# MLP down projection: from 7 products over 2x2 blocks to 20 products over 3x4 by 4x2 blocks, with the weight sums on POOL

## The chip, the cores and the metric

The kernel runs on one NeuronCore of a Trainium2 chip. The metric is the device time of one execution in microseconds (us). The core has a matmul engine (PE; its weight loads are listed as PEld), a vector engine (DVE), a scalar engine (ACT), a general engine (POOL) and SyncE (SP), which issues most of the DMA transfers. Each engine works through its own instruction list in order, and semaphores tie the lists together.

## The reference, cut to what matters

The reference is one step of a small streaming encoder with two layers: 1024 prompt tokens and 8 x 16 = 128 sample tokens, model width 1024, MLP width 4096, all in float32. Each layer has attention and then an MLP with a residual:

```python
def mlp(x, g_norm, w_up, w_down):
    return jnp.square(jax.nn.relu(rmsnorm(x, g_norm) @ w_up)) @ w_down
...
        hp = hp + mlp(hp, g_mlp[layer], w_up[layer], w_down[layer])
        hs = hs + mlp(hs, g_mlp[layer], w_up[layer], w_down[layer])
```

`hp` holds the prompt tokens (eight tiles of 128, numbered 0 to 7), `hs` the sample tokens (one tile, called ST). The change concerns the last product, (1152 tokens x 4096) @ (4096 x 1024), and the form in which its left operand is stored.

## The kernel before, in words

Every float32 product is made of three matmuls on operands that were split in two parts, hi and lo (`mm3`, L725-729: hi x hi, hi x lo, lo x hi). A split (`split`, L106-115) is a cast on ACT (L109) that writes hi, and a subtraction on DVE (L115) that writes lo = value - hi.

Both MLP projections run over blocks with a fast 2x2 scheme: seven block products stand in for eight, at the price of sums of blocks ahead of them (on tokens and on weights) and sums of products behind them. The sample tile is outside the scheme and has plain products.

*Up projection* (`mlp_up`, L759-886). Sixteen blocks of 256 hidden columns. Per block, seven products of 12 matmuls over 512 tokens each, in banks X, Y, Z of PSUM, 24 matmuls for the sample tile, and two transposes of the sample's result. ACT and DVE turn the banks into four quadrants of activations (`e`, tiles named `hc`: hidden half x token half, 128 x 512 each). `combos` (L718-723) makes four sums of quadrants on DVE, and POOL's queue stores seven token operands in DRAM (`hd`, L886), and the sample's split transpose (`h8d`, L825).

*Down projection* (`mlp_down`, L888-1105). Four stages of four blocks each. In a stage, SP loads four raw weight quarters (tiles `r`, 128 x 2048, L949-959) and seven token operands (tiles `s`, three buffers), each of which is split by ACT and DVE. DVE makes four sums of weight quarters in place (L1061, L1063, L1076, L1093). The split weights lie in `w`, three buffers. A product is 4 token tiles x 4 k x 3 = 48 matmuls of 512 columns; the sample tile adds four products of 12 matmuls a stage. Results go from PSUM to the residual tiles `x` by DVE additions (L1033). In the last stage tiles 0 to 3 and ST are stored after the third pair of products, and tiles 4 to 7 after the last product. Layer 0 stores them in `xd`, from where the next layer's attention loads them.

The order of the instructions on each engine comes from a scheduler that sorts by dependencies, buffers and priorities; `follow` and `behind` pin the order of PE's products and of the first loads of a down projection. The first loads have raised priority, so that they go out during the up projection's last blocks. In the down projection PE, ACT, DVE and SP work; POOL has nothing to do there.

Of the kernel before, what the change touches and what calls it, by code (L numbers as in the profile page):

```python
# [8 lines left out]
F32 = mybir.dt.float32  # L9
# [21 lines left out]
HB = 11  # L31
RORDER = (0, 1, 5, 2, 3, 6, 4)
# [43 lines left out]
class Build:  # L76
# [682 lines left out]
    def mlp_up(self, layer, sx, x8, rp, raw0):  # L759
        nc = self.nc  # L760
        tt = nc.vector.tensor_tensor
        with ExitStack() as st:
# [56 lines left out]
            def turn(b, h8):  # L819
# [3 lines left out]
                h8t = hp.tile([P, 2, 2, P], F32R, tag="h8t", name="h8t")  # L823
# [3 lines left out]
            def tokens(blk, quad, ws, e, c, with_sample):  # L827
                w = c.stop - c.start
                v = [z[:, c] for z in e]
# [33 lines left out]
                if with_sample:  # L863
                    turn(blk, h8)
# [10 lines left out]
            for b in range(NFB):  # L875
                quad, ws = weights(b)
                e = [hp.tile([P, 512], F32, tag="h", name="hc", bufs=HB) for _ in range(4)]
                if b == 0:
                    tokens(b, quad, ws, e, slice(0, 256), False)
                    tokens(b, quad, ws, e, slice(256, 512), True)  # L880
                else:
                    tokens(b, quad, ws, e, slice(0, 512), True)
                s = [hp.tile([P, 512], F32, tag="h", name="hs", bufs=HB) for _ in range(3)]
                self.combos(*e, [s[0], s[1], e[2], s[2]])
                for p, z in enumerate((e[0], e[1], e[3], s[0], s[1], e[2], s[2])):
                    nc.gpsimd.dma_start(self.hd[b // 4][:, p, b % 4], z)  # L886

    def mlp_down(self, layer, out):  # L888
        nc = self.nc
        tt = nc.vector.tensor_tensor  # L890
        wd = self.ins["w_down"][layer].rearrange("(b h p) n -> h p b n", h=2, p=P)
        with ExitStack() as st:
            self.psum_pools(st, f"dn{layer}", dict(y=(4, 1), x=(4, 1)), dict(x="x", y="y"))
            kinds = dict(
                s=([P, 2, 4, 512], F32R), w=([P, 2, 4, 512], F32R), h=([P, 4, 2, 2, P], F32R),
                r=([P, 4, 512], F32), p=([P, 4, D], F32),
            )
            homes = {}
# [5 lines left out]
            slots = {}  # L904

            def place(name, *tags, side=None):
                pool = self.pool(st, f"d{name}{layer}", side=side)
                for t in tags:
                    homes[t] = pool
                    slots[t] = fresh(t)  # L910

# [3 lines left out]
            for n, tags in enumerate((("p0",), ("w2",), ("s2",), ("r5", "r6"), ("h8",), ("s1",), ("w1",), ("s0",))):  # L915
                place(f"e{n}_", *tags, side="right")
            place("a", "w0", "r1")
            place("b", "r2")
            place("c", "r3")
            place("d", "r4")  # L920
            xp = self.pool(st, f"dx{layer}")
            xs = {}
            for t in range(NT // 2, NT):
                xs[t] = xp.tile([P, D], F32, tag=f"x{t}", name="x")
            self.bias_tiles(xp)
            xp.tile([P, 504], F32, tag="pad", name="pad")
            place("g", "r0")
            yp = self.pool(st, f"dy{layer}")
            for t in (ST, 0, 1):
                xs[t] = yp.tile([P, D], F32, tag=f"x{t}", name="x")  # L930
            yp = self.pool(st, f"dz{layer}")
            for t in (2, 3):
                xs[t] = yp.tile([P, D], F32, tag=f"x{t}", name="x")

            self.pe = self.sp = None
            self.nr = 0

            def take_raw():
                self.nr += 1
                return take(f"r{RORDER[(self.nr - 1) % 7]}")  # L940

            N = [slice(0, 512), slice(512, 1024)]
            ns = NFB // 4
            count = 0
            for s in range(ns):
                b = [[None, None], [None, None]]
                svs = {}

                def load(dst, src):  # L949
                    a = nc.sync.dma_start(dst, src)  # L950
                    if s == 0:
                        if self.sp is not None:
                            self.behind(self.sp, a)
                        self.sp = a

                def load_b(h, n):
                    r = take_raw()
                    load(r, wd[h, :, s * 4 : s * 4 + 4, N[n]])
                    b[h][n] = r

                def load_s(p):
                    nonlocal count
                    z = take(f"s{count % 3}")
                    svs[p] = z, f"w{(count + (count >= 9) + (count >= 16)) % 3}"
                    count += 1
                    load(z[:, 1].bitcast(F32), self.hd[s][:, p])

                def wsplit(p, src):
                    w = take(svs[p][1])
                    self.cut = self.split(w[:, 0], w[:, 1], src)  # L970
                    return w[:, 0], w[:, 1]

                def ssplit(p):
                    z = svs[p][0]
                    self.cut = self.split(z[:, 0], z[:, 1], z[:, 1].bitcast(F32))
                    return z[:, 0], z[:, 1]

                def load_x(*ts):
                    for t in ts if s == 0 else ():
                        load(xs[t], self.xd[t])  # L980

                if layer == 0 and s == 1:
                    self.prep_bias(self.dp)
                def load_h():
                    h8 = take("h8")
                    for q in range(4):
                        load(h8[:, q].bitcast(F32), self.h8d[s * 4 + q])
                    return h8

                def early(n):  # L990
                    return self.tc.high_priority(n) if s == 0 else nullcontext()

                with early(EARLY[0]):
                    load_b(0, 0)
                    load_x(ST, 0, 1)
                with early(EARLY[1]):
                    load_b(1, 0)
                    load_s(0)
                with early(EARLY[2]):
                    load_s(1)  # L1000
                with early(EARLY[3]):
                    h8 = load_h()
                load_x(2, 3)
                load_b(0, 1)
                load_b(1, 1)
                load_s(4)
                load_x(*range(NT // 2, NT))

                def product(banks, w, sv, first, done):
                    for i in range(4):  # L1010
                        c = slice(i * P, i * P + P)
                        z = [
                            self.mm3(
                                banks[i], sv[0][:, k, c], sv[1][:, k, c], w[0][:, k], w[1][:, k],
                                first and k == 0, k == 3,
                            )
                            for k in range(4)
                        ]
                        self.follow(z[0][0], z[-1][1])
                        done(i)  # L1020

                def sample(ps, w, h, first, last):
                    z = [
                        self.mm3(
                            ps, h8[:, k, 0, h], h8[:, k, 1, h], w[0][:, k], w[1][:, k],
                            first and k == 0, last and k == 3,
                        )
                        for k in range(4)
                    ]
                    self.follow(z[0][0], z[-1][1])  # L1030

                def add(t, n, ps):
                    tt(xs[t][:, N[n]], ps, xs[t][:, N[n]], ALU.add)  # L1033

                def store(t):
                    if s == ns - 1:
                        nc.sync.dma_start(out(t), xs[t])

                bank = lambda role: self.psum(role, [P, 512], f"ps_{role}")
                X = [bank("x") for _ in range(4)]  # L1040
                w = wsplit(0, b[0][0])
                if s == 0:
                    self.behind(self.cut[0], self.marks[0])
                sv = ssplit(0)
                if s == 0:
                    self.behind(self.cut[0], self.marks[1])
                    self.behind(self.cut[1], self.marks[2])
# [33 lines left out]
                def third(i):  # L1081
                    add(i, 1, Y[i])
                    store(i)
# [723 lines left out]
```

## Time and profile before

| | us |
|---|---|
| median of 3 runs | 2393.08 |
| range of the runs | 2387.11 to 2398.38 |
| span of the profiled execution, first to last instruction | 2386.1 |
| time of the profiled execution itself | not listed apart; the lowest run is 1.0 above its span |
| DVE busy in the span | 1627.6 |
| ACT busy in the span | 1216.5 |
| POOL busy in the span | 540.8 |

The stages in the span, by the first matmul of each kind: the down projection of layer 0 begins at 802.2 us and that of layer 1 at 2033.2 us; attention of layer 1 lies between about 1150 and 1650 us. A row of a group of instructions reads: line of the kernel, engine, operation, output <- inputs, shapes, count | busy time in us, mean ns of one | idle time of the engine just ahead of them in us, and what ended it. A row of a timeline reads: start in us, duration in us, engine, line, operation, output <- inputs, shapes, count, and in brackets the idle time ahead of it. Matmul durations of 389 ns overlap, so PE's pace is read from the number of matmuls in a stretch.

### The profile page before, as it was taken

To read this page: it belongs to the slowest core of one execution; us is meant where nothing else is said; L and a number is where in the kernel's file an instruction comes from. 1 tells how busy PE (TensorE), PEld (TensorE's weight loads), DVE (VectorE), ACT (ScalarE), POOL (GpSimd) and SP (SyncE) were. 2 spreads that over 40 slices of the span, in tenths; PEclk is the share of its full clock that TensorE was granted. 3 is DMA by queue.
4 is the path that set the end of the run, shared out by engine and by line. 5 is a ranking of instruction groups with operands and counts; after the bars stand their busy time and mean duration, and the time that the engine had idled before them with its cause. 6 is when DMAs were issued, how large, how long until landed. Compare 5 with 4: busy or idle time off the path is not lost.

```text
span 2386.1 us, 33438 instructions
## 1 busy us (share of the span) xinstructions
PE 2313.9 (97%) x11621; PEld 1931.7 (81%) x11621; DVE 1627.6 (68%) x3002; ACT 1216.5 (51%) x2423; POOL 540.8 (23%) x828
## 2 busy tenths in 40 slices
PE   7998999899999999999999999998999999999999
PEld 6787877788888878888778788887888888888887
DVE  6788786655565776776577876877555565777674
ACT  3777674555555432332267666665555555323321
POOL 4334332311221100000333444444111211000000
PEclk9999999999999999999999999999999999999999
DMA  7335545343443964333653655554443445734332
GB/s 258 119 108 169 170 146 200 129 146 126 157 146 123 356 213 149 119 128 109 232 153 112 198 166 167 168 168 169 142 142 129 158 145 203 274 133 159 117 113 115
DMA packets 217529, 383.78 MB, mean 161 GB/s; under 512 B 50248, under 2 KB 124944, under 8 KB 210192
## 3 DMA queue, kind: packets, MB, share of 16 engines
q1 hardware_dynamic: 194288, 305.08, 38.9%
q0 software_dynamic: 21776, 71.84, 7.8%
q10 hardware_dynamic: 1296, 4.72, 0.5%
q8 instruction: 92, 1.51, 0.3%
q14 instruction: 77, 0.63, 0.1%
HBM read 245.42 MB, written 135.09 MB: 159 GB/s over the span
## 4 chain that ended last, share of the span: by engine, by line
PE 79%; DVE 7%; DMA 7%; ACT 3%; issue 2%; POOL 1%; SPq 1%; ACTq 0%; DVEq 0%; POOLq 0%
PE ps_x L727 9%; PE ps_x L729 9%; PE ps_x L728 9%; PE ps_y L729 7%; PE ps_y L728 7%; PE ps_y L727 7%; PE ps_mm L198 3%; PE ps_mm L200 3%; PE ps_mm L199 3%; PE ps_tr L305 2%; PE ps_mm L157 1%; PE ps_mm L158 1%; PE ps_mm L159 1%; PE ps_s L729 1%; PE ps_s L728 1%
## 5 line engine op out<-in xcount | busy, mean ns | idle before, releaser
L109 ACT CAST w<-r 128x2048 fp32r<-128x2048 f32 x56 | 107.1, 1913 | 325.2 <-PE ps_y L729 213.0
L727 PE MATMUL ps_x<-w,s 128*128 128x512 f32 x512 | 199.6, 390 | 4.2 <-DVE hc L866 2.1
L729 PE MATMUL ps_x<-w,s 128*128 128x512 f32 x512 | 199.4, 389 | 0.0
L728 PE MATMUL ps_x<-w,s 128*128 128x512 f32 x512 | 199.3, 389 | 0.0
L198 PE MATMUL ps_mm<-w,hh 128*128 128x512 f32 x432 | 172.5, 401 | 7.3 <-POOL w L166 3.2
L200 PE MATMUL ps_mm<-w,hl 128*128 128x512 f32 x432 | 172.1, 399 | 1.6 <-DVE hl L115 0.8
L199 PE MATMUL ps_mm<-w,hh 128*128 128x512 f32 x432 | 170.9, 397 | 1.3 <-DVE w L171 1.1
L109 ACT CAST s<-s 128x2048 fp32r<-128x2048 f32 x56 | 107.1, 1913 | 118.1 <-DMA s<-hd 109.3
L115 DVE TENSOR_TENSOR w<-r,w 128x2048 fp32r<-128x2048 f32 x56 | 128.2, 2290 | 51.0 <-ACT w L109 51.0
L727 PE MATMUL ps_x<-sx,w 128*128 128x512 f32 (+1 forms) x408 | 157.9, 387 | 3.9 <-ACT hc L846 3.0
L1033 DVE TENSOR_TENSOR x<-ps_y,x 128x512 f32<-128x512 f32 x136 | 92.4, 687 | 100.8 <-PE ps_y L729 100.8
L729 PE MATMUL ps_x<-sx,w 128*128 128x512 f32 (+1 forms) x408 | 154.2, 378 | 0.0
L728 PE MATMUL ps_x<-sx,w 128*128 128x512 f32 (+1 forms) x408 | 154.1, 378 | 0.0
L109 ACT CAST w<-ru 128x512 fp32r<-128x512 f32 (+1 forms) x160 | 110.0, 708 | 85.5 <-PE ps_y L728 32.0
L729 PE MATMUL ps_y<-w,s 128*128 128x512 f32 x384 | 149.5, 389 | 0.0
L727 PE MATMUL ps_y<-w,s 128*128 128x512 f32 x384 | 149.4, 389 | 0.0
L728 PE MATMUL ps_y<-w,s 128*128 128x512 f32 x384 | 149.4, 389 | 0.0
L115 DVE TENSOR_TENSOR s<-s 128x2048 fp32r<-128x2048 f32 x56 | 128.0, 2286 | 29.1 <-ACT s L109 28.9
L115 DVE TENSOR_TENSOR ptl<-ps_tr,pth 128x512 fp32r<-128x512 f32 x180 | 122.5, 685 | 24.1 <-ACT pth L109 17.8
L115 DVE TENSOR_TENSOR w<-ru,w 128x512 fp32r<-128x512 f32 (+1 forms) x160 | 126.5, 793 | 11.2 <-ACT w L109 11.1
L115 DVE TENSOR_TENSOR wq<-ru,wq 128x1024 fp32r<-128x1024 f32 x32 | 39.7, 1240 | 131.9 <-ACT wq L109 131.9
L109 ACT CAST pth<-ps_tr 128x512 fp32r<-128x512 f32 x180 | 104.9, 595 | 45.0 <-PE ps_tr L305 36.7
(280 smaller groups left out, 6579.7 us busy)
## 6 DMA issues: line engine op xcount, KB each, us to landing
s<-hd SPq DMA_DIRECT2D x56, 1024.0 KB, 4.7
ru<-in_w_up SPq DMA_DIRECT2D x64, 512.0 KB, 4.0
r<-in_w_down SPq DMA_DIRECT2D x32, 1024.0 KB, 5.8
hd<-hc POOLq DMA_DIRECT2D x128, 256.0 KB, 2.7
hd<-hs POOLq DMA_DIRECT2D x96, 256.0 KB, 2.5
x<-xd SPq DMA_DIRECT2D x41, 512.0 KB, 4.4
o<-oTd SPq DMA_DIRECT2D x52, 256.0 KB, 5.0
xd<-xo SPq DMA_DIRECT2D x18, 512.0 KB, 2.8
```

The costliest lines, as they stand in the source:

```text
L109: a = nc.scalar.copy(hi, src)
L115: return a, e.tensor_tensor(lo, src, hi.bitcast(F32), ALU.subtract)
L157: nc.tensor.matmul(ps, oh[:, k, :], w[:, 0, k, nn], start=(k == 0), stop=False)
L158: nc.tensor.matmul(ps, oh[:, k, :], w[:, 1, k, nn], start=False, stop=False)
L198: nc.tensor.matmul(ps, a, w[:, 0, k, :], start=(k == 0), stop=False)
L199: nc.tensor.matmul(ps, a, w[:, 1, k, :], start=False, stop=False)
L200: self.lp = nc.tensor.matmul(ps, b, w[:, 0, k, :], start=False, stop=(k == KC - 1))
L305: self.lp = nc.tensor.transpose(pt[:, i, :], get(i), self.ident)
L727: a = mm(ps, ah, bh, start=first, stop=False, skip_group_check=True)
L728: mm(ps, ah, bl, start=False, stop=False, skip_group_check=True)
L729: return a, mm(ps, al, bh, start=False, stop=last, skip_group_check=True)
L1033: tt(xs[t][:, N[n]], ps, xs[t][:, N[n]], ALU.add)
```

## The change: what it does

1. *The block product of the down projection.* The tokens are cut in three parts of three tiles, (5, 6, 7), (ST, 0, 1) and (2, 3, 4): the sample tile is now an ordinary tile. The hidden dimension is cut in four for each of two sets, the output columns in two. A set makes (3x4) by (4x2) blocks in 20 products where 24 would be plain. Each product is 3 token tiles x 4 k x 3 = 36 matmuls of 512 columns; 40 products a layer.
2. *Token operands.* The up projection writes the activations of a block into two tiles `eh` of 128 x 1152 (ST, then tiles 0 to 7); the sample's transposes are copied there by ACT. After an even block, `forms_even` makes 2 sums and stores 5 operands; after an odd block, `forms_odd` makes 16 sums and stores 15; each is 128 x 384. The sums write in place of tiles that were stored before, where they can. All stores stay on POOL's queue.
3. *Weight operands.* A product uses one raw weight block or the sum or difference of two (16 of 20 in a set). The sums are made on POOL into two buffers (`s0`, `s1`), or in place for the last four; there are two buffers for split weights (`w0`, `w1`), three for tokens (`a0` to `a2`), eleven for raw weights.
4. *Order and PSUM.* Products are grouped in chains (`CHAINS`) that accumulate in the same three banks. Between products of a chain the banks are read, with plus or minus, into the output blocks that need the value at that point. Ahead of the products a loop issues loads three products early, the splits one early, the weight sum two early.
5. *Memory.* The buffers of the down projection have a new fixed order in SBUF (`DOWN_HOME`).

The core of the diff (tables, `forms_odd` and the loading helpers shortened):

```diff
-HB = 11
-RORDER = (0, 1, 5, 2, 3, 6, 4)
+RANK = 20
+PARTS = ((5, 6, 7), (ST, 0, 1), (2, 3, 4))
+COLS = (2, 0, 1)
+W_FORMS = (
+    "+.......", ".......+", "+......-", ".+.....+", ".....+..",
...
+CHAINS = (
+    ((4,), (0, 10), (14, 15), (-13, 18), (12, 1, 2, 17, 9, 8), (-6, 5, 11, 3, 7), (16, 19)),
+    ((0,), (-4, 15), (-14, 10), (-13, 18), (19, 16), (12, 1, 2, 17), (-6, 5, 11, 7, 3), (9, 8)),
+)
...
-                self.split(h8t[:, 0], h8t[:, 1], t8)
-                nc.gpsimd.dma_start(self.h8d[b], h8t.bitcast(F32))
+                for h in range(2):
+                    nc.scalar.copy(eh[h][:, 0:P], t8[:, h])
...
-                s = [hp.tile([P, 512], F32, tag="h", name="hs", bufs=HB) for _ in range(3)]
-                self.combos(*e, [s[0], s[1], e[2], s[2]])
-                for p, z in enumerate((e[0], e[1], e[3], s[0], s[1], e[2], s[2])):
-                    nc.gpsimd.dma_start(self.hd[b // 4][:, p, b % 4], z)
+                if b % 2 == 0:
+                    even = eh
+                    self.forms_even(b // 2, eh)
+                else:
+                    self.forms_odd(b // 2, even + eh, hp.tile([P, 3 * 3 * P], F32, tag="h", name="ht", bufs=7))
...
+    def forms_even(self, c, eh):
+        tt, put = self.nc.vector.tensor_tensor, self.form_store(c)
+        a0, a4, a8 = self.form_cut(eh[0])
+        a1, a5, a9 = self.form_cut(eh[1])
+        put(18, a8)
+        put(3, a0)
+        put(13, a5)
+        tt(a4, a4, a8, ALU.add)
+        put(10, a4)
+        tt(a9, a5, a9, ALU.add)
+        put(11, a9)
...
+            def add_w(n):
...
+                x, y = (raws[used[i][0]] for i in (0, -1))
+                if len(used) == 1:
+                    assert g == 1
+                    src[n] = x
+                    return
+                src[n] = x if n >= total - TAIL + 2 else take(f"s{n % 2}")
...
+                nc.gpsimd.tensor_tensor(src[n], x, y, ALU.add if plus else ALU.subtract)
+
+            def split_w(n):
...
+                w = ws[n] = take(f"w{n % 2}")
+                self.split(w[:, 0], w[:, 1], src.pop(n))
+                a = aa[n]
+                self.split(a[:, 0], a[:, 1], a[:, 1].bitcast(F32))
...
+            add_w(0)
+            split_w(0)
+            add_w(1)
+            for n, (s, p, g, first, final, reads, _) in enumerate(seq):
...
+                split_w(n + 1)
+                add_w(n + 2)
+                if first:
+                    banks = [self.psum("c", [P, 512], "ps_c") for _ in range(3)]
+                a, w = aa.pop(n), ws.pop(n)
+                for i in range(3):
+                    c = slice(i * P, i * P + P)
                     z = [
                         self.mm3(
+                            banks[i], a[:, 0, k, c], a[:, 1, k, c], w[:, 0, k], w[:, 1, k],
+                            first and k == 0, k == 3,
                         )
                         for k in range(4)
                     ]
                     self.follow(z[0][0], z[-1][1])
+                    for o, v in reads:
+                        x = xs[PARTS[o // 2][i]][:, N[o % 2]]
+                        tt(x, x, banks[i], ALU.add if v > 0 else ALU.subtract)
```

More of the change, by code (lines that the diff above doesn't have):

```diff
@@ L863, in tokens @@
                 if with_sample:
-                    turn(blk, h8)
+                    turn(eh, h8)
                 product(Y, 2, False, True)
@@ L917, in mlp_down @@
[L917 to L930, printed above, removed]
@@ L931, in mlp_down @@
-            yp = self.pool(st, f"dz{layer}")
-            for t in (2, 3):
-                xs[t] = yp.tile([P, D], F32, tag=f"x{t}", name="x")
-            self.pe = self.sp = None
[L936 to L982, printed above, removed]
-                    self.prep_bias(self.dp)
[L984 to L1022, printed above, removed]
@@ new lines, in mlp_down @@
+            for n, tags in enumerate(DOWN_HOME):
+                pool = self.pool(st, f"d{n}_{layer}")
+                for t in tags.split():
+                    if t == "bias":
+                        self.bias_tiles(pool)
+                        pool.tile([P, 504], F32, tag="pad", name="pad")
+                    elif t[0] == "+":
+                        pool.tile([P, int(t[1:])], F32, tag="gap", name="gap")
+                    else:
+                        homes[t] = pool
+                        slots[t] = fresh(t)
@@ new lines, in mlp_down, with slot, load @@
+            total = len(seq)
+            left = {}
+            for n, (s, *_, reads, _) in enumerate(seq):
+                for i, _ in reads:
+                    left[i] = n
+            last = {i // 2: max(left[i], left[i ^ 1]) for i in left}
+            aa, ws = {}, {}
+            def slot(n):
+                return 1 + n % 2 if n >= total - TAIL else n % 3
+            def load(dst, src):
+                a = nc.sync.dma_start(dst, src)
+                if self.sp is not None:
+                    self.behind(self.sp, a)
+                self.sp = a
@@ L1030, in sample @@
                     self.follow(z[0][0], z[-1][1])
[L1032 to L1043, printed above, removed]
@@ L1069, in mlp_down @@
-                sv = ssplit(3)
-                s2 = bank("y")
-                sample(s2, w, 0, True, True)
-                add(ST, 1, s2)
-                Y = [bank("y") for _ in range(4)]
-                product(Y, w, sv, True, lambda i: add(i + 4, 1, Y[i]))
-                t4 = b[1][0]
-                tt(t4, b[1][0], t2, ALU.subtract)
-                load_s(6)
-                w = wsplit(6, b[1][1])
-                sv = ssplit(6)
-                def third(i):
-                    add(i, 1, Y[i])
-                    store(i)
@@ L1099, in mlp_down @@
-                sv = ssplit(2)
-                def fourth(i):
-                    add(i + 4, 0, X[i])
-                    store(i + 4)
-                product(X, w, sv, False, fourth)
+                    for o, v in reads:
+                        x = xs[PARTS[o // 2][i]][:, N[o % 2]]
+                        tt(x, x, banks[i], ALU.add if v > 0 else ALU.subtract)
+                    for part in {o // 2 for o, _ in reads}:
+                        if last[part] == n:
+                            t = PARTS[part][i]
+                            nc.sync.dma_start(out(t), xs[t])
@@ L1107, in bias_tiles @@
+                for m in range(n + 1, total):
+                    if m not in aa:
+                        if slot(m) in {slot(q) for q in range(n + 1, m)}:
+                            break
+                        load_h(m)
     def bias_tiles(self, pool):
```

201 lines of the change are left out of this document (137 added, 64 removed).

## The prediction

> **What bounds the kernel now.** I read the page first, then stretches of the down projection one by one, then the groups of instructions there.
>
> ```profile
> span 2386.1 us, 33438 instructions
> PE 2313.9 (97%) x11621; PEld 1931.7 (81%) x11621; DVE 1627.6 (68%) x3002; ACT 1216.5 (51%) x2423; POOL 540.8 (23%) x828
> ```
>
> PE is busy 97% of the span, but that is an average, and its 389 ns matmuls overlap. The two stretches of 200 us below lie inside the down projections of layer 0 and 1; columns are start:end, length, then busy time (count) of PE, PEld, DVE, ACT, POOL, granted clock, DMA share, GB/s.
>
> ```profile
> 900.00:1100.00 200.00, 200.00 (x884) 165.68 (x883) 139.58 (x118) 61.27 (x32) 0.00 (x0) 1.00 0.37 126
> 2090.00:2290.00 200.00, 200.00 (x884) 165.58 (x884) 143.27 (x119) 62.81 (x33) 0.00 (x0) 1.00 0.39 137
> PE ps_x L727 <- DVE x L1033: 2.0, 1, 2.0
> ```
>
> 884 matmuls in 200 us at clock 1.00 are 0.2262 us each: here PE issues without a gap, POOL does nothing, DVE is busy 70 to 72%. The last row, from the list of waits of layer 0's down projection, is PE's only wait in it, 2.0 us. So in this stage PE's matmul count is the time, as long as nothing else needs more than PE.
>
> ```profile
> L729 PE MATMUL ps_x<-w,s 128*128 128x512 f32 x512 | 199.4, 389 | 0.0
> L729 PE MATMUL ps_y<-w,s 128*128 128x512 f32 x384 | 149.5, 389 | 0.0
> L729 PE MATMUL ps_y<-w,h 128*128 128x512 f32 x128 | 49.8, 389 | 0.0
> ```
>
> L727, L728 and L729 have equal counts, so both layers issue 3 x (512+384+128) = 3072 matmuls, 1536 a layer: 347.5 us.
>
> **The change, part by part.**
>
> *Matmuls.* 40 products a layer (two sets of 20), each 3 token tiles x 4 k x 3 = 36 matmuls of the same shape: 1440. The built order of the changed kernel has 192 fewer for both layers. 192 x 0.2262 = **-43.4 us**, if PE stays fed. One product now lasts 36 x 0.2262 = 8.14 us instead of 10.86.
>
> *What feeds a product.* Durations:
>
> ```profile
> L115 DVE TENSOR_TENSOR w<-r,w 128x2048 fp32r<-128x2048 f32 x56 | 128.2, 2290 | 51.0 <-ACT w L109 51.0
> L115 DVE TENSOR_TENSOR s<-s 128x2048 fp32r<-128x2048 f32 x56 | 128.0, 2286 | 29.1 <-ACT s L109 28.9
> L1033 DVE TENSOR_TENSOR x<-ps_y,x 128x512 f32<-128x512 f32 x136 | 92.4, 687 | 100.8 <-PE ps_y L729 100.8
> L1033 DVE TENSOR_TENSOR x<-ps_x,x 128x512 f32<-128x512 f32 x128 | 87.0, 685 | 42.6 <-PE ps_x L729 42.0
> L1061 DVE TENSOR_TENSOR r<-r,r 128x2048 f32<-128x2048 f32 x8 | 18.3, 2283 | 0.0
> L720 DVE TENSOR_TENSOR hs<-hc 128x512 f32<-128x512 f32 x32 | 22.1, 692 | 70.6 <-ACT hc L801 70.6
> L109 ACT CAST w<-r 128x2048 fp32r<-128x2048 f32 x56 | 107.1, 1913 | 325.2 <-PE ps_y L729 213.0
> 919.21 1.91 ACT L109 CAST w<-r 128x2048 fp32r<-128x2048 f32 x1 [9.51 <-PE ps_y L729]
> 921.15 2.29 DVE L115 TENSOR_TENSOR w<-r,w 128x2048 fp32r<-128x2048 f32 x1 [1.25 <-ACT w L109]
> 923.36 0.68 DVE L1033 TENSOR_TENSOR x<-ps_x,x 128x512 f32<-128x512 f32 x1
> ```
>
> The timeline rows show that a successor starts 0.08 before the recorded end, so a weight split holds DVE 2.21, a PSUM read 0.61. From 512 to 2048 elements DVE grows by (2.286-0.692)/1536 = 1.038 ns an element, so a token split of 1536 takes 1.755 recorded, 1.68 in a row. Written out, the chains read the banks for 41 output blocks a layer, three tiles each: 123 reads (136 + 128 for both layers before, 132 a layer). DVE then needs 40 x (2.21+1.68) + 123 x 0.61 = 231 us a layer against PE's 325.8: 71%, as now. ACT needs 40 x (1.91+1.44) = 134 us, the 1.44 again by size. Neither is the bound by itself.
>
> *Sums on POOL.* Sixteen DVE sums a layer (L1061, L1063, L1076, L1093, 2.28 us) go; 32 sums of 128x2048 arrive on POOL, which before did nothing here. The trace has no POOL sum of that size; the nearest:
>
> ```profile
> L684 POOL TENSOR_TENSOR s<-x,s 128x512 f32<-128x512 f32 x6 | 7.7, 1286 | 0.1
> L550 POOL TENSOR_TENSOR uks<-kc,uks 128x128 fp32r<-128x128 f32 x32 | 16.7, 521 | 1.7
> ```
>
> (1.286-0.521)/384 = 1.99 ns an element gives 1.286 + 1536 x 1.99 ns = 4.35; I take 4.4. Ends: 2.28, DVE's own row for that shape, and 4 x 1.286 = 5.14, no fixed cost at all. The Trainium skill, GPSIMD Engine Reference, section 3.1, states 4497 ns for a fp32 sum of N=2048; by it the sum below would end some 5 us later.
>
> *What the two engines do to each other.* This decides the forecast. Around the first MLP's start both work on SBUF (POOL rows, then DVE rows, of the timeline):
>
> ```profile
> 411.50 1.76 POOL L683 TENSOR_TENSOR s<-x 128x512 f32<-128x512 f32 x1
> 414.98 1.29 POOL L684 TENSOR_TENSOR s<-x,s 128x512 f32<-128x512 f32 x1
> 422.56 1.30 POOL L681 TENSOR_TENSOR s<-x 128x512 f32<-128x512 f32 x1
> 423.81 2.28 POOL L683 TENSOR_TENSOR s<-x 128x512 f32<-128x512 f32 x1
> 412.02 0.68 DVE L665 TENSOR_TENSOR x<-ps_wo,x 128x512 f32<-128x512 f32 x1
> 415.05 2.30 DVE L622 SCALAR_TENSOR_TENSOR x<-x,mrs,gb 128x1024 f32<-128x1024 f32 x1
> 420.90 1.28 DVE L622 SCALAR_TENSOR_TENSOR x<-x,mrs,gb 128x1024 f32<-128x1024 f32 x1
> 422.69 2.24 DVE L622 SCALAR_TENSOR_TENSOR x<-x,mrs,gb 128x1024 f32<-128x1024 f32 x1
> ```
>
> L622 takes 1.28 alone. Begun at 415.05 under the POOL sum of 414.98 to 416.27 it ends at 417.35, 1.08 after POOL: it stood still until POOL was done. At 422.69 the same happens under the sum of 422.56, and then the next POOL sum, due at 423.81, stands until that DVE instruction ends at 424.93 and takes 2.28 in place of 1.29. The read of a PSUM bank at 412.02, with one SBUF input, runs at its 0.68 inside a POOL sum. So POOL's sum and a DVE instruction with two SBUF inputs exclude each other for their whole length; a blocked DVE instruction saves 0.2 of its start. The Trainium skill, SBUF — State Buffer, section "Who interferes with whom", makes it a rule: the two-input DVE instruction and a GpSimd instruction that reads SBUF hold a shared read port whole, first come; by it a sum of 2048 blocks as wholly as the 512 ones here, and the rows agree.
>
> Both splits on DVE have two SBUF inputs. In the changed build, DVE's order in a period is: weight split of product n+1, read of product n's first bank, token split of n+1, reads of banks two and three. POOL's sum for n+3 waits for just that weight split, because it frees one of two buffers (s0, s1). So POOL starts while DVE does the read, and the token split, which PE needs for n+1, stands behind the sum; behind it stand two thirds of the reads, and behind those the next weight split. With r output blocks read per tile, a period with a sum is 2.21 + 4.4 + 1.5 (1.68 less 0.2) + 2r x 0.61 = **8.1 + 1.2 r us** (for r = 0 the token split goes ahead of POOL, same sum), against PE's 8.14. Of the 40 products 8 have r = 0, 23 have r = 1, 9 have r = 2. Excess over PE if each period had a sum: 23 x 1.2 + 9 x 2.4 = 49 us; 32 of 40 do: **+39.4 us a layer**. Port time, 32 x 4.4 + 40 x 3.9 = 297 us, would fit under PE's 325.8; it is the order that costs.
>
> A layer's down projection: 325.8 + 39.4 = 365 for 347.5, +17.7; both, **+35 us**.
>
> *Sums of tokens in the up projection.* Per pair of blocks 18 sums of 128x384 (0.692 - 128 x 1.038 ns = 0.56) replace 8 of 0.69 and two 0.42 splits of the sample: +3.7 us of DVE in a pair, +59 for both layers.
>
> ```profile
> L115 DVE TENSOR_TENSOR h8t<-ps_t,h8t 128x256 fp32r<-128x256 f32 x32 | 13.4, 417 | 0.0
> 550.00:600.00 50.00, 50.00 (x247) 42.21 (x246) 27.93 (x43) 27.88 (x46) 9.77 (x18) 1.00 0.43 146
> hd<-hc POOLq DMA_DIRECT2D x128, 256.0 KB, 2.7
> s<-hd SPq DMA_DIRECT2D x56, 1024.0 KB, 4.7
> ```
>
> DVE is idle 22 of 50 us there under a full PE, which hides it: 0. Without that cover it is up to +59. Several new sums overwrite a tile that a store on POOL's queue must first have read (2.7 us to land); queued behind them are the next block's weight splits, which have until that block's end, and the 22 idle us are their slack. POOL issues 20 stores a pair for 16 now, idle otherwise. SP's loads: 40 of 768 KB for 28 of 1024, the weights' 16 unchanged; at 4.7 us for the bigger one, within an 8.14 us period: 0.
>
> *Ends of the stage.*
>
> ```profile
> 802.16 0.50 PE L727 MATMUL ps_x<-w,s 128*128 128x512 f32 x1 [1.06 <-DVE hc L866]
> ```
>
> The stage opens now after a 1.06 us wait. In the changed order two POOL sums lie among the last stores and DVE's last token sums: between 0 and 8.8 a layer, I take 3: +6. Tiles of layer 0 are stored from product 32 of 40 on, earlier than now: -2, between -5 and 0.
>
> **Sum.** 2386.1 + 35 + 6 - 2 = 2425 of span. No time of its own is given for the profiled execution; its span stands 7.0 below the runs' median of 2393.1. Forecast **2432 us**.
>
> **Rivals.**
> 1. *PE sets the pace* (the other side, faster). If POOL's sums run in DVE's gaps, 43 of gain less 4 at the ends leave 2354. It decides at a sum of T < 8.14-2.21-1.5-1.2 = 3.2 us, or if DVE's token split gets in before POOL. For: the port total fits. Against: both POOL rows point to 4.4, and the sum's release is the instruction just before. 0.17.
> 2. *Half absorbed*: sums slip into periods of single-term products and r = 0; excess 20 a layer, about 2393. 0.13.
> 3. *Heavier*: sums of 5.14 add 0.74 to each of 32 periods, +47, or the up projection loses part of its cover: 2480. 0.09.
> 4. *The product count does not fall*: excluded by the built order.
>
> **How the numbers follow.** Forecast 0.61, by itself 2410 to 2460 (sums of 4.0 to 4.8). The range leaves out rival 1 and the heaviest part of rival 3: 2385 to 2472. About 0.5% is what a measurement of this kernel tells from no change: faster 0.18, same 0.13, slower 0.69.
>
> **What would show it.** Right: 40 products of 36 matmuls, but some 790 matmuls in 200 us of the down projection, not 884; PE waiting there for DVE's token split, some 40 us a layer; that split recorded at 4 to 5 us on average in place of 1.76, the PSUM read still 0.69; POOL sums of 4.4 or longer. Wrong: 884 matmuls per 200 us and token splits near 1.8 (rival 1), POOL sums under 3.2, or PE waits in the up projection (rival 3).

## The result, and the profile after

The changed kernel takes 2471.68 us (median of 4 runs, 2465.16 to 2474.45) where the kernel before took 2394.69 on the same chip: 1.033 times as long, 95% interval 1.0304 to 1.0355. The forecast was 2432. The direction is as forecast, and so is the exclusion between POOL and DVE, but the loss is twice the size: +79 us at that ratio instead of +39. The time lies at the very end of the stated range of 2385 to 2472.

The head of the page, and below it the same two stretches of the down projections as before (same columns):

```profile
span 2472.3 us, 33316 instructions
...
PE 2311.3 (93%) x11429; PEld 1911.4 (77%) x11429; DVE 1848.3 (75%) x3128; ACT 1273.0 (51%) x2503; POOL 914.6 (37%) x956
```

```profile
900.00:1100.00 200.00, 178.56 (x767) 143.76 (x765) 184.09 (x105) 75.64 (x45) 101.09 (x20) 0.99 0.39 129
2090.00:2290.00 200.00, 175.11 (x722) 140.37 (x721) 172.28 (x117) 69.73 (x41) 88.07 (x27) 0.93 0.40 139
```

767 and 722 matmuls where 884 were; 790 had been forecast. DVE went from 70% to 92% busy in the first stretch with fewer instructions (105 for 118): they last longer. A look at each down projection from its first matmul to its last, in the same view, gives the whole loss:

```profile
803.60:1196.80 393.20, 343.70 (x1440) 274.72 (x1439) 340.56 (x238) 135.61 (x88) 183.39 (x60) 0.97 0.47 159
2079.10:2467.50 388.40, 346.32 (x1440) 278.54 (x1439) 335.81 (x216) 132.53 (x82) 173.59 (x46) 0.95 0.40 139
sum 781.60, PE 690.02 PEld 553.26 DVE 676.37 ACT 268.14 POOL 356.98; mean PE 345.01 PEld 276.63 DVE 338.19 ACT 134.07 POOL 178.49
```

The same view of the kernel before:

```profile
802.16:1150.20 348.04, 346.00 (x1528) 285.96 (x1528) 245.17 (x212) 101.39 (x56) 7.92 (x12) 1.00 0.47 165
2033.20:2381.50 348.30, 348.29 (x1536) 288.21 (x1536) 237.73 (x201) 100.49 (x54) 1.94 (x4) 1.00 0.41 148
```

So the two grew by 45.2 and 40.1, and the span by 86.2 (of the two profiled executions; the medians on one chip are 77 apart). Little else moved: the first down projection starts at 803.6 instead of 802.2.

The groups of instructions, shapes kept apart, and the list of PE's waits over the whole span (waited in total, times, longest):

```profile
L1067 POOL TENSOR_TENSOR s<-r,r 128x2048 f32<-128x2048 f32 x56 | 291.2, 5202 | 281.2 <-DVE w L134 160.4 <-DMA r<-in_w_down 116.7 <-PE ps_c L748 2.2
L134 DVE TENSOR_TENSOR a<-a 128x1536 fp32r<-128x1536 f32 x80 | 258.5, 3232 | 46.4 <-ACT a L128 46.4
L134 DVE TENSOR_TENSOR w<-s,w 128x2048 fp32r<-128x2048 f32 x56 | 176.3, 3150 | 21.8 <-ACT w L128 21.7
L1119 DVE TENSOR_TENSOR x<-x,ps_c 128x512 f32<-128x512 f32 x246 | 158.8, 676 | 35.7 <-PE ps_c L748 35.5
```

```profile
PE ps_c L746 <- DVE x L1119: 54.7, 25, 6.0
PE ps_c L747 <- DVE w L134: 23.9, 9, 4.2
...
PE ps_c L746 <- ACT a L128: 7.1, 4, 2.5
PE ps_c L748 <- DVE a L134: 5.4, 6, 1.1
```

A token split lasts 3.23 us on average instead of the 1.755 worked out for one alone, a weight split 3.15 instead of 2.29, and the PSUM read, with one input from SBUF, is unchanged at 0.676. That is the exclusion of the prediction, but not always at the place that it named, and so not the 4 to 5 us for a token split: in the timeline 34 of the 80 token splits last over 2.2 us, and 24 of the 80 weight splits over 2.6. But PE hardly waits for token splits (5.4 us); it waits for PSUM reads and weight splits, 78.6 us.

One period of it, DVE and then POOL in the timeline:

```profile
1043.57 5.45 DVE L134 TENSOR_TENSOR w<-s,w 128x2048 fp32r<-128x2048 f32 x1
1048.94 0.67 DVE L1119 TENSOR_TENSOR x<-x,ps_c 128x512 f32<-128x512 f32 x1
1049.54 5.80 DVE L134 TENSOR_TENSOR a<-a 128x1536 fp32r<-128x1536 f32 x1
1055.26 1.27 DVE L1119 TENSOR_TENSOR x<-x,ps_c 128x512 f32<-128x512 f32 x2
1056.46 2.28 DVE L134 TENSOR_TENSOR w<-s,w 128x2048 fp32r<-128x2048 f32 x1
```

```profile
1040.91 5.96 POOL L1067 TENSOR_TENSOR r<-r,r 128x2048 f32<-128x2048 f32 x1
1049.10 4.62 POOL L1067 TENSOR_TENSOR s<-r,r 128x2048 f32<-128x2048 f32 x1 [2.23 <-DVE w L134]
```

The sum starts at 1049.10, the token split, due at 1049.54, stands until 1053.72 and ends at 1055.34; behind it come two reads, of banks that PE's next chained product needs back. The sum by itself is 4.62, for 4.4 taken; the 5.20 of the group holds POOL's own waits too. (The Trainium skill, GPSIMD Engine Reference, section 3.1, states 4497 ns; the trace is 0.12 longer.) At 1040.91 it is POOL that waits, and its late sum then blocks the weight split of 1043.57, which lasts 5.45.

### The profile page after: what moved, and what is told of

It is laid out like the page before. It is cut to its first block, busy times and chain, and to the rows that moved or that the text cites. A ratio compares the mean times of both kernels' runs of the same rounds, so it can differ in the third digit from the quotient of the medians.

```text
span 2472.3 us, 33316 instructions
## 1 busy us (share of the span) xinstructions
PE 2311.3 (93%) x11429; PEld 1911.4 (77%) x11429; DVE 1848.3 (75%) x3128; ACT 1273.0 (51%) x2503; POOL 914.6 (37%) x956
## 4 chain that ended last, share of the span: by engine, by line
PE 62%; DVE 18%; DMA 9%; issue 6%; ACT 3%; POOL 1%; SPq 0%; DVEq 0%; ACTq 0%; POOLq 0%
DVE a L134 5%; PE ps_x L746 5%; PE ps_x L748 5%; PE ps_x L747 5%; DVE w L134 3%; DMA a<-hd 3%; DVE x L1119 3%; PE ps_mm L217 3%; PE ps_c L746 3%; PE ps_c L747 3%; PE ps_c L748 3%; PE ps_mm L219 3%; PE ps_mm L218 3%; PE ps_y L748 2%; PE ps_y L747 2%
## 5 line engine op out<-in xcount | busy, mean ns | idle before, releaser
L746 PE MATMUL ps_c<-w,a 128*128 128x512 f32 x960 | 386.3, 402 | 62.2 <-DVE x L1119 54.7
L747 PE MATMUL ps_c<-w,a 128*128 128x512 f32 x960 | 385.0, 401 | 24.0 <-DVE w L134 23.9
L1067 POOL TENSOR_TENSOR s<-r,r 128x2048 f32<-128x2048 f32 x56 | 291.2, 5202 | 281.2 <-DVE w L134 160.4
L748 PE MATMUL ps_c<-w,a 128*128 128x512 f32 x960 | 383.1, 399 | 5.4 <-DVE a L134 5.4
L911 POOL DMA_DIRECT2D hd<-h x272 | 147.9, 544 | 582.4 <-ACT h L820 280.0
L134 DVE TENSOR_TENSOR a<-a 128x1536 fp32r<-128x1536 f32 x80 | 258.5, 3232 | 46.4 <-ACT a L128 46.4
L746 PEld LDWEIGHTS ps_c<-w,a 128*128 128x128 f32 x960 | 185.9, 194 | 113.7 <-DVE x L1119 36.9
L747 PEld LDWEIGHTS ps_c<-w,a 128*128 128x128 f32 x960 | 185.9, 194 | 67.6 <-DVE w L134 29.4
L128 ACT CAST a<-a 128x1536 fp32r<-128x1536 f32 x80 | 118.5, 1481 | 213.9 <-DMA a<-hd 213.8
L748 PEld LDWEIGHTS ps_c<-w,a 128*128 128x128 f32 x960 | 186.0, 194 | 47.1 <-DVE a L134 8.0
L128 ACT CAST w<-s 128x2048 fp32r<-128x2048 f32 x56 | 107.1, 1912 | 212.0 <-PE ps_c L748 177.9
L134 DVE TENSOR_TENSOR w<-s,w 128x2048 fp32r<-128x2048 f32 x56 | 176.3, 3150 | 21.8 <-ACT w L128 21.7
L1119 DVE TENSOR_TENSOR x<-x,ps_c 128x512 f32<-128x512 f32 x246 | 158.8, 676 | 35.7 <-PE ps_c L748 35.5
L134 DVE TENSOR_TENSOR w<-ru,w 128x512 fp32r<-128x512 f32 (+1 forms) x160 | 126.6, 793 | 15.2 <-ACT w L128 15.1
```

Of the source, the lines that this page charges most:

```text
L128: a = nc.scalar.copy(hi, src)
L134: return a, e.tensor_tensor(lo, src, hi.bitcast(F32), ALU.subtract)
L746: a = mm(ps, ah, bh, start=first, stop=False, skip_group_check=True)
L747: mm(ps, ah, bl, start=False, stop=False, skip_group_check=True)
L748: return a, mm(ps, al, bh, start=False, stop=last, skip_group_check=True)
L911: return lambda p, z: self.nc.gpsimd.dma_start(self.hd[c // 4][:, p, c % 4], z)
```

## The experiments

The theory at this point had two parts: the exclusion costs some 46 to 51 us a layer from the fifth product on, and the start of the stage, 16 us a layer over the first four products, has a cause of its own on SP's queue, as in these rows of SP, POOL and ACT in layer 0:

```profile
800.40 33.69 SPq L1031 DMA_DIRECT2D x<-xd  x3
834.50 0.32 SPq L1031 DMA_DIRECT2D a<-hd  x1
```

```profile
830.59 0.54 POOL L911 DMA_DIRECT2D hd<-ht  x1 [2.46 <-DVE ht L968]
```

```profile
840.77 1.47 ACT L128 CAST a<-a 128x1536 fp32r<-128x1536 f32 x1 [18.74 <-DMA a<-hd]
```

Three loads of residual tiles hold SP for 33.7 us. In the built program tiles 6 and 7 lie in the memory of the last token forms (`ht`), and POOL's last store of those forms is issued only at 830.59 and lands at 833.08; SP's next load goes out at 833.26. The token load of a product stands behind them on the queue, and ACT waits 18.7 us for it. Rivals: DVE is simply full; or it is the amount of POOL work that counts, not its place.

The table has all runs. "Stage" is the length of both down projections together, "PE busy" PE's busy time in it; 80 products at 8.16 us, the shortest seen, would be 653. "Over" is what products take above 8.16 us, from the first matmul of one to that of the next in the timeline, layer 0 / layer 1. Ratios are to the kernel before on the same chip. The four columns behind the ratio come from one profiled execution each; that of e6 is 8 us above its median, the others lie within 7 of theirs.

| kernel | median us | ratio (95%) | stage | PE busy | over, products 1-4 | over, 5-40 |
|---|---|---|---|---|---|---|
| changed kernel | 2471.7 | 1.033 (1.0304-1.0355) | 781.6 | 690.0 | 15.7 / 16.3 | 51.4 / 46.0 |
| e9 sum behind token split | 2470.5 | 1.0346 (1.0327-1.0365) | 778.5 | 692.8 | 16.3 / 22.4 | 53.3 / 34.1 |
| e3 tiles late | 2457.4 | 1.0277 (1.0257-1.0298) | 767.4 | 690.4 | 12.8 / 11.4 | 45.0 / 45.8 |
| e10 sum behind next split | 2439.6 | 1.0209 (1.0194-1.0224) | 747.6 | 682.0 | 19.7 / 16.2 | 31.4 / 27.8 |
| e11 quarters | 2424.4 | 1.0143 (1.0127-1.016) | 735.6 | 683.2 | 15.1 / 13.7 | 30.3 / 24.3 |
| e4 halves | 2421.1 | 1.0129 (1.0105-1.0152) | 732.8 | 678.3 | 17.3 / 13.2 | 29.2 / 20.9 |
| e12 halves, tiles late | 2405.2 | 1.006 (1.004-1.008) | 717.3 | 674.8 | 10.0 / 10.0 | 26.9 / 18.0 |
| e1 sums on DVE | 2399.9 | 1.0032 (1.0017-1.0047) | 709.9 | 673.3 | 15.2 / 15.3 | 18.1 / 8.9 |
| e6 sums on DVE, tiles late | 2376.7 | 0.9958 (0.9942-0.9973) | 691.0 | 667.0 | 6.3 / 5.6 | 19.0 / 7.8 |
| e2 no sums | 2377.9 | 0.9947 (0.9928-0.9966) | 686.1 | 662.9 | 11.4 / 11.1 | 9.0 / 2.1 |
| e7 no sums, tiles late | 2349.3 | 0.9844 (0.9827-0.9861) | 661.5 | 655.4 | 1.0 / 1.0 | 5.2 / 1.9 |
| e8 before, sums on POOL | 2384.0 | 0.9987 (0.9977-0.9997) | | | | |

### e1: the sums on DVE

```diff
-                nc.gpsimd.tensor_tensor(src[n], x, y, ALU.add if plus else ALU.subtract)
+                nc.vector.tensor_tensor(src[n], x, y, ALU.add if plus else ALU.subtract)
```

> The 64 weight sums (32 a layer) go from POOL to DVE; all else is as in the changed kernel. Lock theory (a POOL sum and a DVE split exclude each other whole, and the excess of products 4 to 39, 51 us in layer 0 and 46 in layer 1, comes from it): DVE then needs 231 + 32 x 2.28 = 304 us a layer under PE's 326, periods of products with two reads per tile go over by 1.6 us at most (up to 10 us a layer), so 2360 to 2395 us, token splits back at 1.75 us and PE at 8.2 us a product from the fifth on. Head theory (the order of the loads at the start delays the rest): the 16 us ahead of the third product stay whole, 2440 or more. Rival that DVE is simply full: with more work on DVE the time grows, over 2480.

2399.9, a little above the range of the lock theory; 71 us come back by the ratios, though DVE got 64 more sums. The groups (eight sums in place are left out):

```profile
L134 DVE TENSOR_TENSOR a<-a 128x1536 fp32r<-128x1536 f32 x80 | 140.5, 1757 | 54.2 <-ACT a L128 54.2
L134 DVE TENSOR_TENSOR w<-s,w 128x2048 fp32r<-128x2048 f32 x56 | 128.1, 2287 | 15.8 <-ACT w L128 15.8
L1067 DVE TENSOR_TENSOR s<-r,r 128x2048 f32<-128x2048 f32 x56 | 127.8, 2285 | 4.2 <-DMA r<-in_w_down 4.0
```

Both splits are back at their lengths alone, 1.757 and 2.287. "DVE is full" falls as the cause of the loss. The 15 us at the start stay whole, as the head theory had it, though its time of 2440 or more did not come.

### e2: no sums

```diff
-                if len(used) == 1:
-                    assert g == 1
+                if True:
                     src[n] = x
                     return
```

> Leaves the weight sums out altogether: each product uses the first of its raw weight blocks alone, so the output is another one; loads, splits, products and reads are all there. Lock theory: products 4 to 39 run at PE's 8.14 us, that is 97 us less over both layers, 2355 to 2378, and what is left over 326 us a layer is the head, 8 to 16 us. If the excess came from the loads or from DVE's own amount of work, it stays: over 2440.

2377.9, at the top of the lock theory's range. The sums are worth 1.033 - 0.9947, or 92 us, over both layers. (Without a sum a product does not wait for its second raw block either. That wait is in the 92, and this run does not tell it apart; e1, which keeps it, gave 71 back with the sums' own time on DVE.) Products 10 to 36 take 8.16 us each, but for 0.8 us in all; 11 us a layer stay at the start, with this on SP's queue and POOL's last store ahead of it:

```profile
802.06 27.19 SPq L1031 DMA_DIRECT2D x<-xd  x3
```

```profile
825.79 0.54 POOL L911 DMA_DIRECT2D hd<-ht  x1 [0.39 <-DVE ht L968]
```

The store is issued 4.8 us earlier than with sums, and SP gets on at 829.25 instead of 834.09, again 3.5 us behind it. So the stand at the start is there without any POOL sum; sums only lengthen it.

### e3: residual tiles 5 to 7 loaded three products later

```diff
-X_AT = {0: 2, 1: 1, 3: 0}
+X_AT = {0: 2, 1: 1, 6: 0}
```

> Only the loads of residual tiles 5 to 7 are issued three products later on SP's queue, so that the token loads of products 4 to 6 no longer stand behind them; sums stay on POOL. Head theory (16 us a layer at products 1 to 3 come from SP's queue standing at the loads of these tiles, which wait for POOL's last stores): 10 to 16 us less a layer, 2440 to 2455, and ACT's wait of 18.7 us for the token operand of the third product is gone. Lock theory alone: 2472, since POOL's sums stay as they are; the same time if the raw weights, late as well, end last in that place.

2457.4: 14 us less at the medians, 2 above the expected range. SP no longer stands at these loads, but now DVE does, in the same place (DVE, then POOL, in the timeline):

```profile
829.96 5.74 DVE L134 TENSOR_TENSOR a<-a 128x1536 fp32r<-128x1536 f32 x1
```

```profile
829.53 4.56 POOL L1067 TENSOR_TENSOR s<-r,r 128x2048 f32<-128x2048 f32 x1 [1.08 <-DVE w L134]
```

One wait had hidden the other: with POOL's sums in place the queue is worth only 14 us.

### e4 and e11: each sum in two halves, in four quarters

```diff
-                nc.gpsimd.tensor_tensor(src[n], x, y, ALU.add if plus else ALU.subtract)
+                for k in range(0, 4, 2):
+                    nc.gpsimd.tensor_tensor(
+                        src[n][:, k : k + 2], x[:, k : k + 2], y[:, k : k + 2],
+                        ALU.add if plus else ALU.subtract,
+                    )
```

For quarters the loop runs over all four k, with slices of one.

> Each POOL sum of 128x2048 is issued as two of 128x1024, 2.3 to 2.5 us each. Lock theory, whole instructions and first come: the token split gets in between the halves, so a period with a sum is 2.21 + 2.4 + 1.5 + 2.4 = 8.5 us with one read per tile in place of 9.7 or more: 20 to 35 us less a layer, 2400 to 2430; blocked splits of some 4 us in place of 5.8. Rival (the two engines share the port by bytes, or POOL is slowed in proportion, so that only the amount counts): no change, 2465 to 2480.

> Each POOL sum as four of 128x512, 1.29 us each by the rows of before, so 5.2 us in place of 4.6; all else as in the changed kernel. Lock theory, whole instructions and first come: a DVE instruction is blocked 1.3 us at most, but the two engines need 32 x 5.2 + 40 x 3.9 = 322 us of exclusive time a layer under PE's 326, so quarters win nothing more than halves did (2421): 2400 to 2430. Rival (only the longest single block counts): 2375 to 2395.

2421.1 and 2424.4, both in the range of whole-instruction exclusion. More POOL instructions and the same amount of data give 45 to 50 us back, where the rival by amount had no change. Quarters add nothing to halves. Their groups show what may stand in the way:

```profile
L1068 POOL TENSOR_TENSOR s<-r,r 128x512 f32<-128x512 f32 x224 | 464.3, 2108 | 81.3 <-DMA r<-in_w_down 62.1 <-DVE w L134 17.4 <-issue 1.8
...
L128 ACT CAST w<-s 128x2048 fp32r<-128x2048 f32 x56 | 107.0, 1910 | 236.5 <-POOL s L1068 161.4 <-DVE x L1123 51.3 <-PE ps_c L748 23.7
```

A quarter of a sum now lasts 2.11 us, because POOL stands behind DVE's splits in between. A whole sum takes 4 x 2.11 = 8.4 us, more than a product's 8.16, and ACT waits 161 us for POOL. Part of the wait has changed sides; how much of the time it decides was not measured apart.

### e6 and e7: tiles late, with the sums on DVE and without sums

Both have the edit of e3, on top of e1 and e2.

> Weight sums on DVE and the loads of residual tiles 5 to 7 three products later, both together. With the sums on DVE alone 15 us a layer were left at products 1 to 4, where ACT waited 17 us for the token operand of the third product behind those loads on SP's queue. Queue theory: with no POOL sum to take the place of that wait, 6 to 11 us a layer go, 2378 to 2388, which is level with or a little under the kernel before. Rival (DVE, full of sums and token forms at the start, ends last there anyway): at most 3 us a layer, 2394 to 2400.

> Leaves the weight sums out, as the second experiment did (the first raw block stands in for each), and loads residual tiles 5 to 7 three products later. What is left over PE's 326 us a layer is then the price of the start and the end without any sum. Queue theory: the 11 us a layer at products 1 to 4 fall to 3 to 6, 2362 to 2370. Rival (POOL's stores of the last forms, the last of them at 825 us, or the raw weights end last): over 2374.

e6: 2376.7, 23 us under e1 at the medians and 18 by the ratios. Of the versions with the new block product and its sums it is the only one under the kernel before, by 0.4% (interval 0.9942 to 0.9973), which is less than the 0.5% that the prediction took as the least to be told from no change. Its stretches:

```profile
900.00:1100.00 200.00, 195.91 (x854) 160.84 (x854) 186.55 (x143) 80.03 (x48) 0.00 (x0) 0.99 0.41 142
2090.00:2290.00 200.00, 199.14 (x877) 164.05 (x876) 185.41 (x144) 82.11 (x49) 0.00 (x0) 1.00 0.42 142
```

854 and 877 of 884 matmuls with DVE at 93%: DVE's amount of work is not what costs the changed kernel its 79 us, though it is not free (by the ratios e6 is 27 us above e7, which has no sums). e7, 2349.3, came out below its expected range (2362 to 2370): without sums the queue is worth 29 us at the medians and 24 by the ratios. What products take over 8.16 us falls from 33.6 to 9.1 in both layers, and PE is fed at 655.4 of 661.5 us. e7 leaves the sums out, so it is no version to use; it shows what the product count could give if the sums cost nothing.

### e8: the kernel before, with its sixteen sums a layer on POOL

```diff
-                tt(t1, b[0][1], b[0][0], ALU.subtract)
+                nc.gpsimd.tensor_tensor(t1, b[0][1], b[0][0], ALU.subtract)
```

and the same for the other three sums.

> The kernel before, with its sixteen weight sums a layer moved from DVE to POOL and nothing else. Port theory by amount (a POOL sum costs its length wherever it stands): 16 x 1.6 us and more a layer over PE, 2440 or later. Lock theory, where only what stands behind a blocked split in an order without slack is paid: a product is 10.86 us, DVE needs some 52 us of a stage of 87, three buffers of split operands stand between, so blocked splits of 5 to 6 us are seen but 0 to 12 us a layer are paid, 2390 to 2418.

2384.0, 0.9987 (0.9977 to 0.9997): nothing is paid, and the time is under the expected range. Yet the blocking is there, in its groups and its stretch:

```profile
L115 DVE TENSOR_TENSOR s<-s 128x2048 fp32r<-128x2048 f32 x56 | 191.6, 3421 | 34.6 <-ACT s L109 34.5
...
L1061 POOL TENSOR_TENSOR r<-r,r 128x2048 f32<-128x2048 f32 x8 | 36.9, 4608 | 300.6 <-DVE w L115 267.1 <-DMA h<-h8d 33.5
```

```profile
900.00:1100.00 200.00, 200.00 (x884) 165.61 (x883) 148.42 (x110) 61.25 (x32) 40.97 (x9) 1.00 0.36 126
```

Token splits last 3.42 us instead of 2.29, POOL's sums 4.61 in this group, and PE has 884 matmuls. So a blocked split can cost nothing. This kernel differs from the changed one in several ways at once: half as many sums, three buffers of split weights for two, products of 10.86 us for 8.14. Which of them gives the slack was not tested.

### e9 and e10: the sum waits for a token split

```diff
-                nc.gpsimd.tensor_tensor(src[n], x, y, ALU.add if plus else ALU.subtract)
+                z = nc.gpsimd.tensor_tensor(src[n], x, y, ALU.add if plus else ALU.subtract)
+                if n - 2 in lows:
+                    self.tc.add_manual_dep(z.ins, lows[n - 2].ins.name, WAIT, reason="order")
```

`lows[n]` is the token split of product n; e10 has n - 1 in place of n - 2.

> The changed kernel, with one wait more: each POOL sum waits for the token split that follows the weight split which frees its buffer. The sums stay on POOL and as long as they are, only their phase changes. By the formula of the prediction with the order turned round, a period with a sum is 2.0 + 0.61 r + 1.68 + 4.6 = 8.3 + 0.61 r us in place of 8.3 + 1.2 r, since the reads of the second and third bank lie under POOL: 15 to 22 us a layer less, 2425 to 2445, with the weight split blocked (5 to 6 us) and the token split near 1.76. Rival (phase does not matter, only how long both engines hold the port): 2465 to 2480.

2470.5: no change, a miss. The reason is in the order of the built instructions (buffer numbers kept). On DVE, and then which operands PE's products take together:

```
DVE L134  w1_9428<-s1_9379,w1_9428
DVE L1119 x5_8908<-x5_8908,ps_c_9381
DVE L134  a1_9426<-a1_9426
PE  L746  ps_c_9381<-w1_9428,a0_9371
PE  L746  ps_c_9381<-w0_9476,a1_9426
```

The token split behind weight split w1 is a1, which belongs to the product *after* the one that uses w1. Tokens are split a product further ahead than weights. e9 had tied the sum to a0, long done, so that the order in time hardly changed: 37 token splits still last over 2.2 us. e10 ties it to a1:

> As the ninth experiment, with the wait on the other token split: the ninth tied a POOL sum to the token split of the same product as the weight split that frees its buffer, and that one already stands ahead on DVE; the one that stands behind, and is blocked, is the token split of the product after. Now the sum waits for that. Phase theory: 0.6 + 1.67 + 4.6 + 2.0 = 8.9 us for a period with one read per tile in place of the 9.7 seen, 9.5 for 11 with two, 15 to 25 us a layer less, 2420 to 2445; token splits near 1.76 and weight splits blocked to 5 us. Rival (only the length of both engines' work counts, not the phase): 2465 to 2480.

2439.6, inside the range of the phase theory: some 30 us less by a wait *added*. DVE in e10's timeline, then POOL:

```profile
1029.30 5.72 DVE L134 TENSOR_TENSOR w<-s,w 128x2048 fp32r<-128x2048 f32 x1
1034.94 0.68 DVE L1121 TENSOR_TENSOR x<-x,ps_c 128x512 f32<-128x512 f32 x1
1035.54 1.75 DVE L134 TENSOR_TENSOR a<-a 128x1536 fp32r<-128x1536 f32 x1
1037.20 1.27 DVE L1121 TENSOR_TENSOR x<-x,ps_c 128x512 f32<-128x512 f32 x2
1038.40 5.74 DVE L134 TENSOR_TENSOR w<-s,w 128x2048 fp32r<-128x2048 f32 x1
```

```profile
1037.36 4.63 POOL L1067 TENSOR_TENSOR s<-r,r 128x2048 f32<-128x2048 f32 x1 [4.49 <-DVE a L134]
```

The token split is at 1.75, the weight split blocked to 5.7, two of the three reads lie under the sum, and a period is 9.1 us (1029.30 to 1038.40) in place of 9.7. Over both layers 4 token splits are left over 2.2 us, and 50 weight splits are over 2.6. The Trainium skill, SBUF — State Buffer, section "Who interferes with whom", says that the order of issue decides which engine is blocked; e9 and e10, with the same operations, agree.

### e12: halves and tiles late

> POOL sums as two halves, and the loads of residual tiles 5 to 7 three products later. With whole sums the later loads gave 14 us over both layers, since POOL's sums took the place of the wait; with sums on DVE they gave 23. Expected between the two, 14 to 23 us under the 2421 of halves alone: 2398 to 2407. If halves leave the locks at the start as they were: 2412 or more.

2405.2, inside the expected range and 16 us under e4. It is the best of the new block product seen with the sums on POOL, and stays 29 us above e6.

## Why the prediction was right in kind and wrong in size

*Matmuls, -43.4, and earlier stores, -2: right.* 1440 matmuls a layer. With neither sums nor queue in the way (e7) the ratio is 0.9844, -37 us on 2393 where -45 was forecast; 9 us over PE's 653 are small waits, half of them at the last four products of a layer, that the forecast did not have.

*Exclusion, +39.4 a layer: right in mechanism; that the size came so near is in part luck.* Sums of 4.62 instead of 4.4 add 0.2 to 32 periods, 6.4 a layer, which makes 45.8. Measured, products 5 to 40 lose 51.4 and 46.0, and without sums 5.2 and 1.9 (e7): 46.2 and 44.1. Wrong was what stands behind the blocked split. "The token split, which PE needs for n+1" belongs to the product after, so PE waits for reads and weight splits. The formula has every sum block a token split; about half of the 64 do, and the others mostly block a weight split or wait themselves. It has no term for matmuls at half clock either (last section). That it still fits is probably because all of these lie in one chain on DVE; this was not tested by itself. e9 was built on the wrong reading and e10 on the right one.

*All sums, 2 x (39.4 + 3) = 84.8:* measured 92 (after against e2, with the limit named there).

*"SP's loads: ... within an 8.14 us period: 0", and with it "Ends of the stage", 3 a layer: the step that failed.* It weighed the transfer (4.2 us in the page after, as expected) and not the order of the queue. Loads of residual tiles wait for POOL's last store of token forms, and everything behind them on SP waits too. In the changed kernel the first four products are 15.7 and 16.3 us over where 3 was forecast, so 26 us of the miss arise there. By itself the queue is worth 24 us over both layers without sums (0.9947 against 0.9844), 18 with sums on DVE (e1, e6), 13 with sums on POOL (e3). That the tiles share memory with the forms could have been read from the built program.

So of the 40 us between 2432 and 2471.7, if the sums are taken out first and then the queue, the queue is some 24, the sums 7, and the small waits 8. In the other order the queue is 13 and the sums, then worth 104 (1.0277 - 0.9844), are 19 over their forecast: both end waits in the same place, and their shares depend on the order.

*Token sums in the up projection, 0: right.* The stage starts 1.4 us later.

*Rivals.* PE sets the pace (2354) needed sums under 3.2 us or the token split ahead of POOL; the sums are 4.62, and with the token split ahead (e10) it is still 2440. "Half absorbed" is excluded by the 46 us a layer. "Heavier" gave 2480, near the time, but for sums of 5.14 or a lost cover in the up projection, and neither is there.

## What to carry to other kernels

A sum moved to an idle POOL isn't always free where DVE has two-input instructions: find what stands behind the blocked one on DVE, and how many buffers lie between it and PE; blocking by 16 sums a layer cost nothing in e8, by 32 some 45 us a layer here. For each load that moves, read what its memory still waits for and what is queued behind it, not only how long its transfer takes. Two waits in one place hide each other, so undo both before either is called cheap.

## What was not expected of the hardware

PE's clock halves behind PE's gaps. A stretch at the start of layer 0's stage in the changed kernel, and in its timeline the two matmuls that end waits there:

```profile
825.00:832.00 7.00, 3.59 (x8) 2.54 (x9) 7.00 (x9) 0.00 (x0) 2.17 (x4) 0.50 0.38 137
```

```profile
825.65 0.76 PE L746 MATMUL ps_c<-w,a 128*128 128x512 f32 x1 [5.57 <-DVE x L1119]
829.17 0.79 PE L747 MATMUL ps_c<-w,a 128*128 128x512 f32 x1 [2.75 <-DVE w L134]
```

The granted clock is 0.50 in the stretch of 7 us, and a matmul behind a wait takes 0.76, where the prediction's row of the stage's opening has 0.50 behind one. (The Trainium skill, TensorE: Matmul & The Clock Gate, Part 1, has the array fall to half clock after an idle window of about 3.4 us; the 5.57 us gap agrees.) Yet a shorter gap was enough later, at 1043 us:

```profile
1043.11 0.71 PE L746 MATMUL ps_c<-w,a 128*128 128x512 f32 x1 [2.48 <-DVE x L1119]
1043.61 0.63 PE L747 MATMUL ps_c<-w,a 128*128 128x512 f32 x1
1044.04 0.63 PE L748 MATMUL ps_c<-w,a 128*128 128x512 f32 x1
```

Behind 2.48 us of waiting the matmuls start 0.43 us apart, about twice the 0.2262 of full clock.

Over both stages PE's busy time for the same 2880 matmuls is 690.0 us in the changed kernel, 673.3 in e1, 655.4 in e7. So a wait can cost more than its own length. How much of the 37 us of slower matmuls between the changed kernel's 690 and 653 lies on the path that sets the end, and how much in time in which PE would have waited for DVE, was not separated.
